# First and last big chunk of 120 rows, eight of them meant for one half of the transfer engines at the front and for the other half at the end

## Chip, cores, metric

One core of one Trainium2 chip. The metric is the time of one execution in microseconds (us), the median of several.

## The reference, cut

```python
pred, target: (8192, 8192) float32; target is 0 or 1
pred = np.clip(pred, eps, 1 - eps)          # eps = 1e-7
return -(target * np.log(pred) + (1 - target) * np.log(1 - pred))
```

Three matrices of 268.4 MB cross between HBM and the core: two are read, one is written.

## The kernel before

The matrices are treated as one flat run of elements, cut into chunks. A big chunk is 128 rows (one for each partition of SBUF) of 15,360 elements; three buffers in a ring hold two big chunks and a remainder. Target is cast to bfloat16 on its way in; its loads, and nearly all others, are issued by GpSimd (POOL). VectorE is DVE in the profile, ScalarE ACT. Of each pair of buffers one is loaded or stored while the other is computed on.

```python
BIG = 15 * 1024
HALF = BIG // 2

def plan(total):                      # (columns, place in the ring) of each chunk
    n, last = divmod(total, BIG)      # n = 34, last = 2048
    spots = [(HALF, 0), (HALF, HALF)]
    spots += [(BIG, k % 2 * BIG) for k in range(1, n - 1)]
    end = (n - 1) % 2 * BIG
    return spots + [(HALF, end), (HALF, end + HALF), (last, 2 * BIG)]
...
def chunk(ap, k):
    flat = ap.rearrange("r c -> (r c)")
    return flat[cols[k] * P : (cols[k] + widths[k]) * P].rearrange("(p w) -> p w", p=P)
...
def load(k):
    queue = nc.sync if k == 0 else nc.gpsimd
    nc.gpsimd.dma_start(out=spot(ring_t, k), in_=chunk(target, k))
    queue.dma_start(out=spot(ring_p, k), in_=chunk(pred, k))

def store(k):
    queue = nc.sync if k >= n - 3 else nc.gpsimd
    queue.dma_start(out=chunk(out, k), in_=spot(ring_p, k))
...
for k in range(2, n - 4):
    front(k, (0, 2)); front(k, (1, 2))      # clip, t-1+p on VectorE; abs, ln on ScalarE
    back(k, (0, 2)); back(k, (1, 2))        # negate on VectorE
    store(k)
    load(k + 2)      # (cut) into the buffer that this store empties; after the loop the tail
```

## Time and profile before

| | before |
|---|---|
| median time | 1866.37 us (1865.87 to 1866.57) |
| busy share of DVE, ACT | 60%, 48% |
| bytes read and written in HBM | 536.87 + 268.44 MB, 432 GB/s over the span |
| two chunks in the steady middle | 108.69 us |

The profile's page gives each engine's busy share in 40 slices of the span; the row DMA is the mean busy share of the sixteen transfer engines. A digit of 9 says that an engine had a packet in hand for over 90% of a slice. The lines themselves stand in the prediction.

### The profile page before, as it was taken

Reading aid. Unit: us, or ns where it says so; the run is one execution under the profiler, and the core shown is the slowest. Engines: PE = TensorE matmul, PEld = TensorE weight load, DVE = VectorE, ACT = ScalarE, POOL = GpSimd, SP = SyncE. Lnnn points to the kernel's source line nnn. Section 1 sums busy time; section 2 is a strip of 40 time slices with the busy share of each in tenths; the row PEclk is TensorE's granted clock in tenths of the full one; section 3 lists DMA queues with packets and bytes.
Section 4 is the critical chain, followed back from the end, with each engine's and each line's share of the span. In section 5 each row is a group of like instructions: output and inputs, shape, how many; then the busy total and the mean of one; then the engine's idle time right before and its main releaser. Section 6 shows DMA issues by size and latency. Waiting matters only on the chain.

```text
span 1864.1 us, 619 instructions
## 1 busy us (share of the span) xinstructions
DVE 1122.2 (60%) x210; ACT 899.9 (48%) x142; POOL 57.5 (3%) x111
## 2 busy tenths in 40 slices
DVE  4655766555576655557665555766555576655585
ACT  3345553335555333555533355553335555333565
POOL 0000000000000000000000000000000000000000
DMA  9999999999999999999999999999999999999999
GB/s 295 374 357 341 353 343 368 383 384 351 347 352 344 371 382 384 348 349 353 347 367 384 382 352 347 353 345 368 385 382 352 345 353 348 365 387 380 353 334 389
DMA packets 15988, 671.13 MB, mean 360 GB/s; under 512 B 1776, under 2 KB 1776, under 8 KB 1904
## 3 DMA queue, kind: packets, MB, share of 16 engines
q0 software_dynamic: 15408, 658.25, 98.5%
q1 hardware_dynamic: 576, 12.85, 1.7%
q14 instruction: 4, 0.03, 0.0%
HBM read 536.87 MB, written 268.44 MB: 432 GB/s over the span
## 4 chain that ended last, share of the span: by engine, by line
DMA 35%; issue 26%; ACT 22%; DVE 15%; POOL 1%; DVEq 0%; POOLq 0%; PEldq 0%
DMA ring_p<-in_pred_dram 32%; ACT ring_p L88 11%; ACT ring_p L89 11%; DVE ring_p L85 7%; DVE ring_p L82 4%; DVE ring_p L93 4%; DMA out_dram<-ring_p 3%; POOL ring_t L73 0%; POOL out_dram L78 0%; DVEq L157 0%; POOL ring_p L74 0%; POOLq L78 0%; POOLq L73 0%; DVEq L82 0%; PEldq L157 0%
## 5 line engine op out<-in xcount | busy, mean ns | idle before, releaser
L88 ACT ACTIVATE ring_p<-ring_p 128x7680 f32<-128x7680 f32 (+1 forms) x70 | 450.6, 6437 | 941.4 <-DVE ring_p L85 941.4
L85 DVE SCALAR_TENSOR_TENSOR ring_p<-ring_t,ring_p 128x7680 f32<-128x7680 bf16 (+1 forms) x70 | 557.2, 7960 | 2.4
L82 DVE TENSOR_SCALAR ring_p<-ring_p 128x7680 f32<-128x7680 f32 (+1 forms) x70 | 284.0, 4057 | 399.0 <-DMA ring_p<-in_pred_dram 399.0
L93 DVE TENSOR_SCALAR ring_p<-ring_p 128x7680 f32<-128x7680 f32 (+1 forms) x69 | 284.0, 4117 | 321.5 <-ACT ring_p L89 321.5
L89 ACT ACTIVATE ring_p<-ring_p 128x7680 f32<-128x7680 f32 (+1 forms) x70 | 451.1, 6444 | 2.2
L74 POOL DMA_DIRECT2D ring_p<-in_pred_dram x36 | 19.3, 535 | 909.2 <-DMA out_dram<-ring_p 909.2
L78 POOL DMA_DIRECT2D out_dram<-ring_p x34 | 18.2, 537 | 851.0 <-DVE ring_p L93 851.0
L73 POOL DMA_DIRECT2D ring_t<-in_target_dram x37 | 20.3, 550 | 0.8 <-PEq L157 0.8
L99 ACT ACT_TABLE_LOAD x1 | 1.3, 1283 | 0.7 <-PEq L146 0.7
L96 DVE MEMSET warm<- 1x8 f32 x1 | 0.1, 65 | 0.8 <-PEq L146 0.8
L99 ACT ACTIVATE warm<-warm 1x8 f32<-1x8 f32 x1 | 0.2, 208 | 0.0
L146 POOL MEMSET const-float32-0.0<- 128x1 f32 x1 | 0.1, 98 | 0.2 <-issue 0.2
L146 POOL MEMSET const-bfloat16-1.0<- 128x1 bf16 x1 | 0.1, 101 | 0.0
L146 POOL MEMSET const-uint8-127<- 128x1 uint8 x1 | 0.1, 99 | 0.0
L146 POOL MEMSET const-float32-1.0<- 128x1 f32 x1 | 0.1, 98 | 0.0
## 6 DMA issues: line engine op xcount, KB each, us to landing
ring_p<-in_pred_dram POOLq DMA_DIRECT2D x32, 7680.0 KB, 35.9
out_dram<-ring_p POOLq DMA_DIRECT2D x32, 7680.0 KB, 29.2
ring_t<-in_target_dram POOLq DMA_DIRECT2D x32, 3840.0 KB, 46.8
ring_p<-in_pred_dram POOLq DMA_DIRECT2D x3, 3840.0 KB, 34.9
ring_t<-in_target_dram POOLq DMA_DIRECT2D x4, 1920.0 KB, 27.7
out_dram<-ring_p POOLq DMA_DIRECT2D x2, 3840.0 KB, 27.6
out_dram<-ring_p SPq DMA_DIRECT2D x2, 3840.0 KB, 15.7
ring_p<-in_pred_dram SPq DMA_DIRECT2D x1, 3840.0 KB, 18.8
```

The lines of the kernel that those rows point to most:

```text
L73: nc.gpsimd.dma_start(out=spot(ring_t, k), in_=chunk(target, k))
L74: queue.dma_start(out=spot(ring_p, k), in_=chunk(pred, k))
L78: queue.dma_start(out=chunk(out, k), in_=spot(ring_p, k))
L82: nc.vector.tensor_scalar(out=p, in0=p, scalar1=EPS, scalar2=1 - EPS, op0=Alu.max, op1=Alu.min)
L85: nc.vector.scalar_tensor_tensor(out=p, in0=t, scalar=1.0, in1=p, op0=Alu.subtract, op1=Alu.add)
L88: nc.scalar.activation(out=p, in_=p, func=Act.Abs)
L89: nc.scalar.activation(out=p, in_=p, func=Act.Ln)
L93: nc.vector.tensor_scalar(out=p, in0=p, scalar1=-1.0, scalar2=None, op0=Alu.mult)
L96: nc.vector.memset(warm, 1.0)
L99: nc.scalar.activation(out=warm, in_=warm, func=Act.Ln)
L146: nc = _bacc.Bacc("TRN2", target_bir_lowering=False, num_devices=1)
```

## The change

The intent, as I took it: in the trace of the kernel before, sixteen engines turn from loading to storing at nearly the same moment (their landings lie 1 to 4 us apart), and at the turn at about 72 us the last row of a pred load takes 0.6 to 1.3 us more than the usual 2.27. The guess was that less is lost when one half of them runs ahead of the other. The first big chunk gets 120 rows, 112 for all engines and eight for one half alone; the last big chunk is to give the same extra rows to the other half, so that both have moved the same at the end. The trace of the changed kernel shows the shares at the front: the rows of the 112-row target load start sixteen at a time, seven times over, 2.27 us apart, and the eight rows all start between 54.58 and 55.17 us, one on each of eight engines. The piece of 64 columns was put in so that the eight rows fall to the other half at the end. The remainder chunk takes up the rest and grows from 2048 to 3968 columns.

```diff
+FEW, WHOLE, EVEN = 120, 112, 64
+
+def plan(total, P):
+    n = total // (BIG * P)
+    last = (total - (n * P - 2 * (P - FEW)) * BIG) // P
...
+    for k in (2, n - 1):
+        spots[k] = (FEW, *spots[k][1:])
...
     def load(k):
+        rows, w, _ = spots[k]
+        parts = [(slice(0, rows), slice(0, w))]
+        if rows < P:
+            rest = slice(WHOLE, rows)
+            parts = [(slice(0, WHOLE), slice(0, w))]
+            parts += [(rest, slice(0, w - EVEN)), (rest, slice(w - EVEN, w))]
+        for part in parts:
+            nc.gpsimd.dma_start(out=spot(ring_t, k)[part], in_=chunk(target, k)[part])
         queue = nc.sync if k == 0 else nc.gpsimd
-        nc.gpsimd.dma_start(out=spot(ring_t, k), in_=chunk(target, k))
-        queue.dma_start(out=spot(ring_p, k), in_=chunk(pred, k))
+        for part in parts:
+            queue.dma_start(out=spot(ring_p, k)[part], in_=chunk(pred, k)[part])

     def store(k):
+        rows = spots[k][0]
         queue = nc.sync if k >= n - 3 else nc.gpsimd
-        queue.dma_start(out=chunk(out, k), in_=spot(ring_p, k))
+        for part in [slice(0, rows)] if rows == P else [slice(0, WHOLE), slice(WHOLE, rows)]:
+            queue.dma_start(out=chunk(out, k)[part], in_=spot(ring_p, k)[part])
```

More of the change, by code (lines that the diff above doesn't have):

```diff
@@ L15 @@
 HALF = BIG // 2
-def plan(total):
-    n, last = divmod(total, BIG)
-    assert n > 4 and 0 < last <= 2048
-    spots = [(HALF, 0), (HALF, HALF)]
-    spots += [(BIG, k % 2 * BIG) for k in range(1, n - 1)]
+FEW, WHOLE, EVEN = 120, 112, 64
+def plan(total, P):
+    n = total // (BIG * P)
+    last = (total - (n * P - 2 * (P - FEW)) * BIG) // P
+    assert n > 6 and 0 < last <= 4096
+    spots = [(P, HALF, 0), (P, HALF, HALF)]
+    spots += [(P, BIG, k % 2 * BIG) for k in range(1, n - 1)]
+    for k in (2, n - 1):
+        spots[k] = (FEW, *spots[k][1:])
     end = (n - 1) % 2 * BIG
-    return spots + [(HALF, end), (HALF, end + HALF), (last, 2 * BIG)]
+    spots += [(P, HALF, end), (P, HALF, end + HALF), (P, last, 2 * BIG)]
+    assert sum(r * w for r, w, _ in spots) == total
+    return spots
 @with_exitstack
@@ L50 @@
     R, C = pred.shape
-    spots = plan(R * C // P)
+    spots = plan(R * C, P)
     n = len(spots)
-    widths = [w for w, _ in spots]
-    cols = [sum(widths[:k]) for k in range(n)]
+    sizes = [r * w for r, w, _ in spots]
     def chunk(ap, k):
-        flat = ap.rearrange("r c -> (r c)")
-        return flat[cols[k] * P : (cols[k] + widths[k]) * P].rearrange("(p w) -> p w", p=P)
+        first = sum(sizes[:k])
+        flat = ap.rearrange("r c -> (r c)")[first : first + sizes[k]]
+        return flat.rearrange("(p w) -> p w", p=spots[k][0])
     pool = ctx.enter_context(tc.tile_pool(name="rings", bufs=1))
-    ring = [P, 2 * BIG + widths[-1]]
+    ring = [P, 2 * BIG + spots[-1][1]]
     ring_p = pool.tile(ring, fp32, name="ring_p", tag="ring_p")
@@ L66, in spot @@
     def spot(ring, k, part=(0, 1)):
-        w, c = spots[k]
+        rows, w, c = spots[k]
         i, m = part
-        return ring[:, c + i * w // m : c + (i + 1) * w // m]
+        return ring[:rows, c + i * w // m : c + (i + 1) * w // m]
     def load(k):
+        rows, w, _ = spots[k]
[6 more added lines that the diff above has]
+            nc.gpsimd.dma_start(out=spot(ring_t, k)[part], in_=chunk(target, k)[part])
         queue = nc.sync if k == 0 else nc.gpsimd
-        nc.gpsimd.dma_start(out=spot(ring_t, k), in_=chunk(target, k))
-        queue.dma_start(out=spot(ring_p, k), in_=chunk(pred, k))
+        for part in parts:
+            queue.dma_start(out=spot(ring_p, k)[part], in_=chunk(pred, k)[part])
     def store(k):
+        rows = spots[k][0]
         queue = nc.sync if k >= n - 3 else nc.gpsimd
-        queue.dma_start(out=chunk(out, k), in_=spot(ring_p, k))
+        for part in [slice(0, rows)] if rows == P else [slice(0, WHOLE), slice(WHOLE, rows)]:
+            queue.dma_start(out=chunk(out, k)[part], in_=spot(ring_p, k)[part])
     def front(k, *part):
```

## The prediction

> **What bounds the kernel now.** I read the busy slices first, then the queue totals, then the chain of waits, last the landings.
>
> ```profile
> DVE  4655766555576655557665555766555576655585
> ACT  3345553335555333555533355553335555333565
> ...
> DMA  9999999999999999999999999999999999999999
> ...
> HBM read 536.87 MB, written 268.44 MB: 432 GB/s over the span
> ```
>
> No compute engine is near full (the page gives DVE 60%, ACT 48%), while the sixteen transfer engines are full in every slice. The GB/s row of that part counts the target load at its bfloat16 size on arrival, so it swings; the HBM line counts what is read and written, 805.31 MB, and is the one to use. The kernel is bound by transfer throughput, start to end.
>
> How close is it to the best rate? The chain in order of time passes through every second chunk's load of pred (columns: start us, us, what):
>
> ```profile
> 150.74 37.18 DMA ring_p<-in_pred_dram
> ...
> 260.87 36.41 DMA ring_p<-in_pred_dram
> ...
> 370.09 36.27 DMA ring_p<-in_pred_dram
> ...
> 479.14 35.90 DMA ring_p<-in_pred_dram
> ...
> 1022.70 35.94 DMA ring_p<-in_pred_dram
> ...
> 1131.39 35.92 DMA ring_p<-in_pred_dram
> ```
>
> In the middle two chunks take 1131.39 - 1022.70 = 108.69 us, so one takes 54.35. A chunk moves 128 x 15360 x 4 bytes three times (two reads, one write), 23.59 MB: 434.1 GB/s. All 805.31 MB at this rate take 1855.0 us; the span is 1864.1. So **everything outside the steady rate is 9.1 us**, 0.5% of the time. The early pairs are slower: 110.13, 109.22 and 109.05 us, together 2.3 us over three steady pairs.
>
> The queue never runs dry, which is why no wait in the table of waits costs anything:
>
> ```profile
> POOL ring_p L74 <- DMA out_dram<-ring_p: 909.2, 32, 29.7
> POOL out_dram L78 <- DVE ring_p L93: 851.0, 34, 52.7
> ```
>
> These look large, but while POOL waits for a store to land, the next target load (18.1 us of work, a third of 54.35) already stands behind that store; and pred takes 35.9 us from issue to landing, 18 of them its own, so the queue had 18 us ahead of it. A store is issued 54.35 us after the one before; pred was issued 29.7 us into that stretch and needs 35.9, so about 11 us of it are still queued then. **The slack is 11 us, in the slowest engine's time.**
>
> The last piece is the spread of the engines. Each transfer leaves sixteen landing records in the trace, one for each engine. First to last they lie 1.0 us apart for the first load, 2.9 us by 190 us, 4.0 us from 650 us on, and 3.0 us at the last store; twelve engines stay within about 2 us and four trail. The packet records show where this comes from: a 61,440-byte row takes 2.27 us in the steady state, but the last row of a pred load, ahead of the turn to the store, took 0.6 to 1.3 us more on all sixteen engines at about 72 us of the span, and up to 1.25 us more at 182 us; after some 700 us hardly any row does.[...]
>
> [...] No transfer of the kernel before has fewer than 128 rows[...]. [...] one steady row is 61,440 bytes in 2.27 us, 27.1 GB/s[...].
>
> **The change part by part.** Bytes: the two big chunks lose 8 rows each, the last chunk grows from 2048 to 3968 columns; 805.31 MB stay 805.31.
>
> Split at the front: chunk 2 (the first big one) gives one half of the engines, call it A, 7 + 1 rows per transfer as before, the other, B, 7. B is one row ahead after target (2.28 us), two after pred (4.5 us) and three after the store (6.8 us, 3 x 2.27). It stays 6.8 us ahead through the middle. At chunk z (the last big one) [...] three rows each way, so both halves end with the same sum. Cost in the steady rate: none, as each engine still moves 8 rows per transfer. The lead of 6.8 us fits into the 11 us of queue, though with the 3 to 4 us spread on top only just.
>
> Added issues: 2 + 2 for loads and 1 for the store, in two chunks: 10 by 0.54 us, 5.4 us of POOL time, all behind 18 us or more of queued work: 0 on the path. The 8 x 64 pieces, four of them: small packets of 128 or 256 bytes, one per engine; the packet of 4,096 bytes took 0.32 us in the trace, so at most about 0.3 us each, on one half: some 0.6 us per half at worst.
>
> Compute: an instruction of 120 rows takes what one of 128 does, 4.16 and 8.16 us on DVE and 6.6 on ACT[...]. The last chunk's instructions grow by 3968/2048: front 1.22 + 2.29 to 6.8 us, ACT 1.90 + 1.91 to 7.4 us, back 1.1 to 2.2 us. Is the tail exposed? Before, the last store was ready near 1846 us and the store ahead of it landed at 1851 to 1862, so there is a good 10 us in hand. Half A's z loads are two rows shorter and land 4.5 us sooner, which pulls the tail's compute forward by as much; the added 1920 columns cost about 7 to 8 us on it, leaving about 3 us later with the slack unspent. So 0 on the path.
>
> What it can gain: eight engines instead of sixteen turn from load to store together. If the hold-up scales with how many turn at once, about half of the excess goes. The slowest engine's loss is 9.1 us, less about 1 us until the first packet and 1.7 us from the last landing to the end of the span: 6.4 us. I take a third to a half of this, 2 to 3 us, against 0.6 us for small packets. **Sum: 1866.4 - 2.4 = 1864.0 us.**
>
> **The rivals.** First, [...] The store gate follows the later half and B's lead is capped by 11 us of queue, so the two mostly add: 22 to 32 us, 1888 to 1898 us. [...] two 112-row chunks lose more, and it passes 1904, the 2% line. [...] someone balanced the change so finely by engines that a loss of this size would have been the first thing seen. Second, **nothing happens**: the 4 us spread is already there after 400 us, the engines sort themselves out anyhow, and the last engine still comes last: 1866. Third, **starvation**: B's lead plus its own spread uses up the 11 us, B idles before stores, loses its lead, and pays for it at z with up to 2 to 4 us: 1868 to 1870. Fourth, [...] one half gets the extra row both times: three rows, 6.8 us: 1873.
>
> **Range and chances.** A gain over 2% would need 37 us, where the whole distance to the steady rate is 9.1: 1%. A loss over 2%[...]: 9%. About 7 in 10 for 1860 to 1867, the rest mostly between 1868 and 1898. Range 1859 to 1886.
>
> **What would show it.** Right: steady pairs stay 108.7 us; landings of a middle transfer fall into two groups some 7 us apart, which come together at the end; the first pairs in the chain are shorter than 110.13 and 109.22. [...] chunk 2's pred lands about 9 us later or more after 77 us, its eight-row packets show durations of several us instead of 2.27, and the rows of 112-row transfers show more than 2.27. Starvation: DMA slices under 9 in the middle or pairs over 108.7. [...] the landings at the end keep two groups 7 us or more apart.[...]

## The result, and the profile after

The changed kernel takes **1935.62 us** in the median (1934.59 to 1938.85, five runs), against 1866.37: **3.8% slower**, ratio 1.0376 (95% interval 1.0362 to 1.039). A ratio here is the mean time of one kernel's fast runs over that of the other's fast runs of the same rounds, so not quite the ratio of the medians. The result is correct, and the profiled run lasted 1937.65 us, a span of 1935.8.

First the same parts of the page, after the change:

```profile
DMA  9999999999999999999999999999999999999896
...
q0 software_dynamic: 15632, 657.27, 97.4%
q1 hardware_dynamic: 576, 13.83, 1.8%
...
HBM read 536.87 MB, written 268.44 MB: 416 GB/s over the span
```

where the kernel before has, for the two queues (packets, MB, share of sixteen engines' span),

```profile
q0 software_dynamic: 15408, 658.25, 98.5%
q1 hardware_dynamic: 576, 12.85, 1.7%
```

The bytes are the same, and the engines are as busy as before until near the end, where two slices of 40 are below 9. An engine has packets in hand for 100.2% of 1864.1 us before (packets overlap a little) and 99.2% of 1935.8 after: some 52 of the 71.7 us of longer span are the same bytes carried more slowly. Most of the rest is idle time of engines that are done early at the end.

The chain of waits in order of time (start us, us, what), at the places where the prediction shows it:

```profile
177.89 37.01 DMA ring_p<-in_pred_dram
...
287.64 35.96 DMA ring_p<-in_pred_dram
...
396.47 35.97 DMA ring_p<-in_pred_dram
...
505.27 36.84 DMA ring_p<-in_pred_dram
...
1052.23 36.75 DMA ring_p<-in_pred_dram
...
1161.72 37.02 DMA ring_p<-in_pred_dram
```

The pairs in the middle take 1161.72 - 1052.23 = 109.49 us, not 108.69. Laid beside the moments at which the kernel before issued the same loads of pred, they tell where the time went:

| moment | before, us | after, us | late by |
|---|---|---|---|
| pred load of chunk 10 issued | 479.14 | 505.27 | 26.1 |
| pred load of chunk 32 issued | 1674.83 | 1709.91 | 35.1 |
| pred load of the last big chunk issued | 1729.18 | 1765.27 | 36.1 |
| pred load of the chunk after it issued | 1783.62 | 1832.95 | 49.3 |
| end of the span | 1864.1 | 1935.8 | 71.7 |

So **26 us at the front, 10 in the middle, 36 at the end.**

At the front, the stretches view (columns: stretch and its length, then DVE, ACT and POOL busy, the clock, the DMA busy share and what was moved in GB/s) looks at the pred load of the first big chunk. The first line is the kernel before:

```profile
58.00:74.00 16.00, 4.16 (x1) 7.63 (x2) 1.08 (x2) 1.00 1.05 430
```

and this one the kernel after:

```profile
62.00:84.00 22.00, 4.16 (x1) 3.66 (x1) 1.09 (x2) 1.00 0.95 246
```

The busy share is about 1 in both, the rate falls from 430 to 246 GB/s. Pred is float32 on both sides, so this rate isn't bent by the cast. The packet records of the trace say it for single rows: a row of 61,440 bytes, 2.27 us in the kernel before, takes 4.1 us in this load, in the mean of its 112 rows. The eight-row pieces take 6.8 us a row here, and about 4.0 at the last big chunk.

The timeline at the end (start us, us, engine, line, operation, and in brackets the idle time before it and what ended it) shows the same for the last big chunk:

```profile
1765.27 1.55 POOL L92 DMA_DIRECT2D ring_p<-in_pred_dram  x3 [28.40 <-DMA out_dram<-ring_p]
...
1814.99 4.16 DVE L102 TENSOR_SCALAR ring_p<-ring_p 120x7680 f32<-120x7680 f32 x1 [25.14 <-DMA ring_p<-in_pred_dram]
...
1832.95 0.54 POOL L92 DMA_DIRECT2D ring_p<-in_pred_dram  x1 [41.66 <-DMA out_dram<-ring_p]
```

Its pred, in three pieces, is issued at 1765 and can be used only at 1815, 50 us later, where 36 were usual; the next load of pred waits 41.66 us for a store, 13 more than the 28 that are usual.

**The two halves were not evened out.** In the target loads the rows of the eight-row pieces can be told by their size, 30,592 bytes and 128 bytes for the 64 columns. In both chunks each of the eight small rows starts within 0.05 us of the end of one of the eight larger rows, so the 64 columns went to the same eight engines. At the front these eight land at 59.8 to 61.2 us and the others at 55.2 to 56.5; of the eight-row pred, eight engines land at 93.6 to 95.7 us and the others at 85.1 to 85.9. At the last big chunk eight engines land the 112-row target load within 0.3 us of each other, from 1771.07 on, and have no part in the eight rows; the eight that come after them (two close behind, six late, up to 1781.46) get the rows, and the last ends at 1784.24. So the half that was late got the extra rows again. eight_spread below, where the two groups are clearly apart, shows the same: there the eight rows start at 1759.4 to 1764.2, and the half that leads had landed by 1757.2. The landings of the last store run from 1912.65 to 1934.95 us, which is the idle time at the end. One half so moves all its eight rows in both big chunks, as before, and its share of the wider remainder on top: as much as three rows of 2.27 us more, an estimate of 6.8 of the 69 us; what else the second helping cost, no run shows.

### The profile page after: what moved, and what is told of

Read it like the earlier page. It is cut to its first block, busy times and chain, and to the rows that moved or that the text cites. A ratio compares the mean times of both kernels' runs of the same rounds, so it can differ in the third digit from the quotient of the medians.

```text
span 1935.8 us, 643 instructions
## 1 busy us (share of the span) xinstructions
DVE 1126.2 (58%) x210; ACT 903.3 (47%) x142; POOL 65.6 (3%) x121
## 2 busy tenths in 40 slices
DMA packets 16212, 671.13 MB, mean 347 GB/s; under 512 B 2048, under 2 KB 2048, under 8 KB 2176
## 4 chain that ended last, share of the span: by engine, by line
DMA 36%; issue 25%; ACT 21%; DVE 15%; POOL 1%; POOLq 0%; PEldq 0%
DMA ring_p<-in_pred_dram 32%; ACT ring_p L109 11%; ACT ring_p L108 11%; DVE ring_p L105 7%; DMA out_dram<-ring_p 4%; DVE ring_p L102 4%; DVE ring_p L113 4%; POOL ring_t L89 0%; POOL out_dram L98 0%; POOL ring_p L92 0%; POOLq L98 0%; PEldq L177 0%; POOLq L92 0%
## 5 line engine op out<-in xcount | busy, mean ns | idle before, releaser
L108 ACT ACTIVATE ring_p<-ring_p 128x7680 f32<-128x7680 f32 (+2 forms) x70 | 452.2, 6461 | 992.9 <-DVE ring_p L105 992.9
L105 DVE SCALAR_TENSOR_TENSOR ring_p<-ring_t,ring_p 128x7680 f32<-128x7680 bf16 (+2 forms) x70 | 559.2, 7989 | 2.4
L102 DVE TENSOR_SCALAR ring_p<-ring_p 128x7680 f32<-128x7680 f32 (+2 forms) x70 | 285.0, 4072 | 448.3 <-DMA ring_p<-in_pred_dram 448.3
L113 DVE TENSOR_SCALAR ring_p<-ring_p 128x7680 f32<-128x7680 f32 (+2 forms) x69 | 285.1, 4131 | 323.7 <-ACT ring_p L109 323.7
L109 ACT ACTIVATE ring_p<-ring_p 128x7680 f32<-128x7680 f32 (+2 forms) x70 | 452.7, 6467 | 2.2
L92 POOL DMA_DIRECT2D ring_p<-in_pred_dram x40 | 24.0, 601 | 982.4 <-DMA out_dram<-ring_p 923.1
```

The costliest lines, as they stand in the source:

```text
L92: queue.dma_start(out=spot(ring_p, k)[part], in_=chunk(pred, k)[part])
L102: nc.vector.tensor_scalar(out=p, in0=p, scalar1=EPS, scalar2=1 - EPS, op0=Alu.max, op1=Alu.min)
L105: nc.vector.scalar_tensor_tensor(out=p, in0=t, scalar=1.0, in1=p, op0=Alu.subtract, op1=Alu.add)
L108: nc.scalar.activation(out=p, in_=p, func=Act.Abs)
L109: nc.scalar.activation(out=p, in_=p, func=Act.Ln)
L113: nc.vector.tensor_scalar(out=p, in0=p, scalar1=-1.0, scalar2=None, op0=Alu.mult)
```

## The experiments

Two theories. **Crowding**: how long a row takes depends on which partitions of SBUF it lies on and on which the other engines move rows at that moment; the seven-row shares of rows 0-111, and rows 112-119 above all, would then be slow. This was a guess, and the runs are there to test it. **Rivals**: the pieces as such (more and smaller transfers, waits for reused semaphores), the HBM side (a new order of addresses), and the uneven halves (a lead that upsets the queue). Thirteen kernels ran; all gave correct results. Where an expectation names a rival, the figures ahead of it are those of crowding. The times quoted beside them are those of the kernel before in the same rounds.

### The pieces alone: columns3

Both chunks keep 128 rows; the transfers are cut by columns into as many pieces as in the change.

```diff
+"columns": [(slice(0, P), slice(a, b)) for a, b in ((0, w - 1024), (w - 1024, w - 64), (w - 64, w))]
```

> The kernel before, with the transfers of the first and last big chunk cut into as many pieces as in the change (three per load, two per store, ten more in all), but by columns: every piece keeps all 128 rows. [...] no cost, 1866 to 1868 us. Rival, pieces and semaphores (more and smaller transfers, waits for reused semaphores): most of the change's 69 us, at least 1890 us.

Measured: 1865.80 us against 1866.77. Ten more transfers, small ones among them, cost nothing. The pieces are out.

### Sixty-four rows: rows64_target, rows64_pred, rows64_store

The kernel before, with one kind of transfer of those two chunks cut into rows 0-63 and 64-127, so that the rows of a piece lie on half of the partitions (the run's helper written out):

```diff
-        queue.dma_start(out=spot(ring_p, k), in_=chunk(pred, k))
+        for part in [(slice(0, 64), slice(0, w)), (slice(64, P), slice(0, w))]:    # chunks 2 and n - 4
+            queue.dma_start(out=spot(ring_p, k)[part], in_=chunk(pred, k)[part])
```

> The kernel before, with only the target loads of those two chunks cut into rows 0-63 and 64-127. [...] target arrives as bfloat16[...]: no cost, 1866 to 1868 us, rows stay at 2.28 us. Rival, HBM side (the new order of addresses is slow to read): as much as for pred, +36 us, 1902 us.

> The same cut for the pred loads only, float32 on both sides. [...] a row takes 4.5 us in place of 2.27, a transfer 36 in place of 18: +18.1 us for each of two chunks, 1902 us. Rival, pieces: as for target, one more transfer each: 1866 to 1868 us. Rival, HBM side: the same cost as for target.

> The same cut for the stores only. [...] +36 us, 1902 us, rows of 4.5 us. In the changed kernel the 112-row store was slowed far less than the 112-row pred load (about 19 to 21 us against 28 to 30), so if reads of SBUF are spread more freely: +5 to +15 us. Rival, pieces: 1866 to 1868 us.

Measured, each against 1866.77: target **1867.74** (+1.0), pred **1905.48** (+38.7), store **1903.49** (+36.7). The expected figures were 0, 36 and 36 (5 to 15 for the store, if reads of SBUF were freer). The stretches view of the pred load of the first big chunk in rows64_pred, to be held against the 430 GB/s shown above:

```profile
58.00:94.00 36.00, 4.16 (x1) 7.51 (x2) 1.07 (x2) 1.00 0.93 191
```

of its store in rows64_store:

```profile
130.00:166.00 36.00, 28.71 (x5) 20.66 (x4) 0.00 (x0) 1.00 0.98 224
```

where the kernel before has, for the same store,

```profile
120.00:133.00 13.00, 1.05 (x2) 0.00 (x0) 1.07 (x2) 1.00 1.02 435
```

and of the target load, first in rows64_target,

```profile
40.00:56.00 16.00, 15.97 (x3) 8.74 (x2) 0.00 (x0) 1.00 1.02 215
```

then in the kernel before:

```profile
40.00:56.00 16.00, 15.93 (x3) 8.74 (x2) 0.00 (x0) 1.00 1.00 215
```

In all five the busy share is near 1. The rate halves for float32, reading SBUF as well as writing it (430 to 191, 435 to 224 GB/s), and stays at 215 for target, whose bytes are counted (and arrive) at half size, 30,720 a row. This settles the side for loads: target reads HBM in the same order and bytes as pred and costs 1.0 us, so HBM isn't it. The two differ in what arrives in SBUF. The store writes HBM and has no such control here; eight_spread gives one below. In the packet records a row of the float32 pieces takes 4.79 us, 2.11 times 2.27. Two such rows at once are 2 x 61,440 bytes in 4.79 us, 25.7 GB/s, where one row in the kernel before has 27.1: as if two engines had what one has there (an estimate from these two times; no view shows what they share).

### The change without uneven halves: rows112_all

The kernel before, with all transfers of both chunks cut into rows 0-111 and 112-127: no piece of eight rows.

```diff
+"rows112": [(slice(0, 112), slice(0, w)), (slice(112, P), slice(0, w))]
```

> The kernel before, with target, pred and store of the first and last big chunk cut into rows 0-111 and 112-127: [...] no eight-row piece, no half ahead. [...] nearly the whole loss of the change comes without any imbalance of the halves: the 112-row pred about 13 us over, its store about 4, [...] 33 us a chunk, some 1932 us (1915 to 1940). Rival, the halves (uneven work, a lead that empties the queue): 1866 to 1870 us.

Measured: 1922.46 us against 1866.22, +56.2; expected were 1932 and 1915 to 1940. So a loss of this size needs no uneven halves. It isn't the change less its imbalance, though: its sixteen rows, side by side on partitions 112 to 127, took some 7.6 us each for pred, where a row of the kernel before takes 2.27. It is also free of loss in the middle: late by 25.7 us from chunk 13 to the last big one, without a change.

### Each end alone: front_only, end_only

The change at one of the two chunks; the remainder is 3008 columns wide. With one end alone nothing can even the halves out: one of them moves 3.4 us more than before (an estimate: 960 columns more in the remainder are half a row for each engine, three times 2.27 us by a half).

```diff
-    for k in (2, n - 1):
+    for k in (2,):            # end_only: (n - 1,)
```

> The change at the first big chunk only (the last is whole; the remainder chunk is 3008 wide). [...] from where the changed kernel lost its time (26 us by the fifth chunk, some 10 more in the middle): 1898 to 1908 us. If the middle's 10 us come from the half that is ahead emptying its queue, they are here too, spread evenly over the middle chunks. Rival, only the end costs: 1866 to 1870 us.

> The change at the last big chunk only. [...] 13 us up to the next load and some 20 more to the end, 1895 to 1902 us, and no loss in the middle (pairs of chunks stay at 108.7 us). If the middle's loss came from anything but the lead of one half, it would be here too: 1905 us or more.

Measured against 1866.22: front **1901.92** (+35.7), end **1903.78** (+37.6). They add up to 73.3, near the 69 of both, in which the uneven work adds up too. The middle's loss is in front_only (late by 25 us at the first chunks, by 33 at the last big one) and not in end_only (by 0.2 us up to there), so it comes with the lead of one half.

### The seven-row shares alone: front112

The first big chunk of 112 rows in one piece each way, no eight-row pieces; the remainder takes up the rest, so all engines move what they moved before.

```diff
-FEW, WHOLE, EVEN = 120, 112, 64
+FEW, WHOLE, EVEN = 112, 112, 64      # and each transfer of the chunk in one piece
-    for k in (2, n - 1):
+    for k in (2,):
```

> The first big chunk of 112 rows alone, in one piece each way, without the eight rows; the last big chunk is whole and the remainder chunk 3968 wide. No half is ahead. [...] the seven-row shares alone cost about 13 us on pred and 4 on the store, nothing on target: 1880 to 1886 us, and no loss in the middle (pairs of 108.7 us). Rival, only the eight rows cost: 1866 to 1868 us.

Measured: **1880.13 us** against 1866.29, +13.8, at the lower edge of what was expected; no loss in the middle (late by 8.6 us at chunk 4, by 7.3 to 7.6 from chunk 9 on; the wider remainder then adds some 6.8 at the end). The pred load of that chunk, in the stretches view:

```profile
56.00:82.00 26.00, 5.09 (x2) 10.10 (x2) 1.67 (x3) 1.00 0.93 227
```

It landed 28.2 us after the target load ahead of it, where seven rows need 15.9: 12.3 us. Target was at its usual rate. The store of the chunk was less slowed, as in the changed kernel. So the eight rows and the lead they make account for the other 22 us of front_only (35.7 - 13.8): 8 in the middle, 3.4 of uneven work, which leaves some 10 directly.

### The eight rows on every second partition: eight_spread

The change, with the eight rows on every second partition from 112 on. Compute works on 128 partitions there; what it makes of the unused ones, filled once at the start (cut here), isn't stored.

```diff
+    def seat(rows):
+        return slice(WHOLE, P - 1, 2) if rows.start == WHOLE else rows
```

> The change as it is, but the eight rows lie on partitions 112, 114, ..., 126[...] (the compute works on 128 partitions, eight of them with values that nobody stores). [...] the float32 rows of the eight-row pieces take about 4.5 us instead of 7 to 9, the lead shrinks below 9 us, and with it goes most of the middle's loss: 1905 to 1922 us. Rival, an eight-row piece is slow because only eight engines work in it: no gain, 1933 to 1938 us.

Measured: **1911.27 us** against 1866.29, so 24 us better than the change with the same rows, again on eight engines. At the first chunk the eight-row pieces of pred took 4.0 us a row, those of target 2.5, in place of 6.8 and 3.4. The lead shrinks with them, and the middle loses 3.4 us (late by 16.4 at chunk 10, by 19.8 at the last big one) in place of 10. For the transfers only where the rows lie in SBUF was changed, for the store too: at the first chunk its eight rows landed 2.8 us after the 112-row piece, in place of 6.0, with the same addresses in HBM.

### A lead from rows four partitions apart: late_half_3, late_half_7, late_half_10

The kernel before with small extra loads of pred at the start, into space that nothing reads. Each goes to eight partitions four apart, where the eight rows of the change lie side by side. The extra work for one half is 8, 16 or 24 such loads: 3.5, 6.9 or 10.4 us, an estimate with the 27.1 GB/s of a row in the kernel before.

```diff
+        for first in (0, 1, 2, 3, 32, 33, 34, 35):
+            for late in (spare, ring_p[:, 2 * BIG :]):
+                w = late.shape[1]
+                flat = pred.rearrange("r c -> (r c)")[first * w : (first + 8) * w]
+                nc.sync.dma_start(out=late[first : first + 29 : 4, :], in_=flat.rearrange("(p w) -> p w", p=8))
```

> As late_half_7, with eight extra small loads: 3.5 us more work for one half. If a lead of one half relieves the turns from load to store, the cost stays under the extra work: 1867 to 1869 us. If it relieves nothing: 1870 us.

> The kernel before, with sixteen extra small loads of pred into unused space at the start, eight partitions four apart each[...]: 6.9 us more work for half the engines[...], and never given back. Correct output. If a lead of 6.9 us between halves is harmless in itself: 1873 us, or 1869 to 1872 if it also ends the hold-up at the turns from load to store. If a lead of that size empties the queue of the half that is ahead and bunches its engines: a loss of up to 10 us more in the middle, 1876 to 1884 us, and pairs of chunks over 108.7 us.

> As late_half_7, with 24 extra small loads: 10.4 us more work for one half[...]. If it is the size of the lead (9.6 us of spread in the changed kernel, 8.5 us in late_half_7 without loss) that costs the changed kernel about 0.3 us per middle chunk: 8 to 10 us over the extra work, 1884 to 1887 us, leaders landing within 1 us of each other, pairs of chunks near 109.5 us. If the middle's loss has another cause: 1876 to 1878 us, pairs of 108.7 us.

Measured: 1869.58 (+3.3 for 3.5 of work, three runs between 1868.2 and 1872.6), 1873.01 against 1866.22 (+6.8 for 6.9), 1881.31 against 1866.29 (+15.0 for 10.4). The chain in the middle of late_half_7:

```profile
1027.87 35.95 DMA ring_p<-in_pred_dram
...
1136.56 35.97 DMA ring_p<-in_pred_dram
```

and of late_half_10:

```profile
1035.43 36.74 DMA ring_p<-in_pred_dram
...
1144.91 36.58 DMA ring_p<-in_pred_dram
```

The pairs take 108.69 and 109.48 us. In late_half_7 the two halves land some 7 us apart all through, which is the lead that the change was after, and it costs nothing; nor does it gain anything to speak of. In the middle the kernel is late by 5.2 us rather than 6.9, so 1.7 us are made up there, but the whole time shows 0.1 us of it, less than its two runs differ by (1.6). The third shows the other side: with a lead of 10 us the slow half loses about 7 more in the middle (late by 8.4 us at chunk 5, by 15.4 at the last big one), and the whole is 4.6 us over the extra work, less than the 8 to 10 I had expected. The engines aren't idle meanwhile (the DMA share between 700 and 1200 us is 1.00 in the changed kernel and in late_half_10, as before). Their rows take longer now and then, up to 3.3 us, while the leaders land within 1 us of each other. Why the leaders bunch is not shown.

### Crowded rows and the engines that don't move them: late_half_shared

late_half_7 with each small load on eight adjacent partitions. The rows of pred that they read are other ones. The expectation takes three cases in turn: only the half with the extra work is late; the other half is late as well; the partitions don't matter.

```diff
-        for first in (0, 1, 2, 3, 32, 33, 34, 35):
+        for first in (0, 8, 16, 24, 32, 40, 48, 56):
...
-out=late[first : first + 29 : 4, :]
+out=late[first : first + 8, :]
```

> As late_half_7, but each of the sixteen small extra loads goes to eight adjacent partitions [...] instead of eight that lie four apart. [...] the half with the extra work ends it some 20 us later than in late_half_7 [...], while the other half's landings of the first loads stay where they were (29.5 us for the second target half, 38.5 for the second pred half); 1890 to 1900 us. [...] the other half lands those loads late as well, by several us up to some 15, its rows of 1.15 us grow to 1.5 us or more, and the total is again 1886 to 1900 us. [...] 1873 us as in late_half_7.

Measured: **1887.50 us** against 1866.19, so 14.5 us over late_half_7 with as many bytes on eight engines. Some 10 of them arise at the start; the middle adds 5 (late by 15.4 us at chunk 5, by 20.6 at the last big one), as with the longer lead of late_half_10. The landing records (from the span's start; the expectation counts from 0.7 us later): the half without extra work began to land the second half-chunk of pred at 39.3 us in late_half_7 and at 43.9 here, 4.6 us later. The other half had landed at 44.4 and at 54.4. So the crowding held up engines that had no part in the small loads; by what way is not shown. In the 112-row pred load of the changed kernel's first big chunk the rows of all sixteen engines were slow as well, 2.8 us at the least and half of them 4.25 or more; whether for the same reason is not shown, since no run shows which engine took which rows. Why the 112-row store leaves most rows at 2.27 us, when the 64-row store was slowed as much as the load, stays open too.

No run points to a version that beats the kernel before by more than its spread: a lead from rows four partitions apart shows no gain that its runs could tell from none (0.1 to 0.2 us in the medians, where the three runs of late_half_3 lie 4.4 us apart), and columns3 differs by 0.04%, within its interval of 0.9967 to 1.0025.

## Why the prediction was wrong, point by point

**What bounds the kernel: right.** The transfers do, and the time was lost there: 52 us as slower packets, the rest as waiting for the later half at the end.

**"Cost in the steady rate: none, as each engine still moves 8 rows per transfer": the step that failed.** It counts rows per engine and takes it for granted that a row takes 2.27 us wherever it lies. All transfers of the kernel before have 128 rows, as the prediction says, so its trace shows this time for that layout alone; it was used for the others all the same. In the pieces cut by rows it took 4.79 us (rows64_pred, rows64_store), 4.1 in the 112-row pred of the first chunk and 6.8 in its eight-row piece.

**"Three rows each way, so both halves end with the same sum": failed too.** The late half got the rows at both ends. This is the fourth rival, which the prediction gave 6.8 us, and its sign came: the last store's landings lie up to 22 us apart.

**The first rival, crowding: its signs came, but weighed and sized too low.** The signs were rows of several us in the eight-row pieces (6.8) and of more than 2.27 in the 112-row transfers (4.1 for pred). It was put down by an argument, and no view carried that argument. Its sum of 22 to 32 us was the estimate for the eight rows, worked out from no trace; front_only less front112 and the uneven work gives some 10 directly at one chunk. The term that was left without a figure, the seven-row shares, was 13.8 us for one chunk (front112). I had thought of the eight rows and not worked it out for the 112, which are fourteen times as many. The sum of the rival, 22 to 32 us, lacked twice 13.8, the middle's 10 and the 6.8 of uneven work.

**The lead "fits into the 11 us of queue": right for 6.8 us, wrong for what came of it.** The eight rows, at 6.8 us each, made a spread of 9.6 us in the middle instead. A lead of 7 us is free (late_half_7) and one of 10 is not (late_half_10). The starvation rival saw the limit, but put the loss on the leading half, at the end, as idle time. It was the late half's, spread over the middle, with the engines busy: 10 us, not 2 to 4. The sign named for it, pairs over 108.7 us, came (109.49); the other one, slices under 9 in the middle, did not.

**The gain of 2 to 3 us: too high.** None is to be seen in the times (late_half_3, late_half_7). The middle of late_half_7 is late by 1.7 us less than the extra work; whether that is lost again at the end, its two runs can't tell.

**Issues, small pieces and compute "0 on the path": right** for the pieces (columns3). The compute instructions of 120 rows took what those of 128 take, 4.16 and 8.16 us on DVE and 6.6 on ACT. The range failed with the first step: 1935.6 is 50 us above its upper end, in the corner that had a chance of 9%. One reading is off without consequence: the store ahead of the last one landed at 1857.7 to 1860.8 us, not 1851 to 1862.

## What to carry to other kernels

A transfer engine that is "busy" may be moving its packet slowly (0.93 busy at 191 GB/s in rows64_pred, 1.05 at 430 in the kernel before): read the busy share together with the rate, and for a transfer that changes its partitions, measure what a row takes there before counting rows (2.27, 4.79 and 6.8 us here). Where a change rests on which engines take a piece, look in the trace whether they did: here the balance was never there. In a kernel that runs at the transfer limit, keep 128 partitions in each float32 transfer and cut by columns, which was free here (columns3, 1865.80 against 1866.77 us), not by rows, which doubled the time of a row (rows64_pred, 4.79 us). When the trace can't rule a rival out, size all of it and give it a weight to match; an argument on why nobody would have written such a change is no evidence.
